# Attention over pairs of heads: value products of 512 columns, and eight wide buffers for exponentials and for pairs of parts

## The chip, the cores and the metric

The kernel runs on one core of a Trainium2 chip, as one launch. The metric is the device time of one execution, in microseconds (us). Names used below: PE is the matrix engine (TensorE), PEld its weight loads, DVE is VectorE, ACT is ScalarE, POOL is GpSimd, SP is the engine that issues most of the transfers.

## The reference, cut to what matters

One sequence of 1024 positions and 1024 channels goes through two layers in float32. Layer 0 mixes positions by grouped-query attention: 16 query heads of 64 channels share 4 key and value heads, four query heads to each. Layer 1 mixes by a gated unit, and each layer ends with a squared-ReLU MLP.

```python
q = apply_rope(rmsnorm(q.reshape(B, T, N_HEADS, HEAD_DIM), q_g), cos, sin)
k = apply_rope(rmsnorm(k.reshape(B, T, N_KV_HEADS, HEAD_DIM), k_g), cos, sin)
v = v.reshape(B, T, N_KV_HEADS, HEAD_DIM)
...
s = jnp.einsum('bqkgd,bskd->bkgqs', q_blk, k).astype(jnp.float32) * scale
p = jax.nn.softmax(s, axis=-1).astype(v.dtype)
return jnp.einsum('bkgqs,bskd->bqkgd', p, v)
```

## The kernel before, in words

**Precision.** Matrix operands are split into a high part, which the cast to `F32R` keeps, and a low part, the rest. A product of two matrices is then three products (high-high, high-low, low-high), or two where one side stands as a stack of both parts. ACT makes the high part by a copy with a cast, DVE the low one by a subtraction. `split`, `norm_hl` and `wo_prep` make such pairs.

**Memory.** `slot` gives a tile of 128 x 512 from a pool of 58 (tag `t`), `xslot` one of 16 (tag `x`), `wide` one of 128 x 1024; its tag `c` is a part of memory that `cut(4)` or `cut(8)` lays out anew for each stage, as four wide tiles or eight of half the size. A tile is given back after its last reader, and an instruction that is to write into a tile waits until one is free. In PSUM, `bank_x` has four buffers of 128 x 512, and `ps_s` two of 128 x 1024 for scores.

**Attention.** The work is cut into 64 units: a quarter of the queries (256 positions, as two blocks `j` of 128) by one head. The order is quarter `qq`, group `g` (the four heads that share values), head `h4`. For each unit there are these stages:

- `s_stage(u, j)`: 4 products of 512 columns give the scores of 128 queries against 1024 keys; DVE takes the negated maximum of each row (L955).
- `e_stage(u, j)`: ACT takes the exponential with that bias, into a wide buffer of tag `c`, and sums the rows (L961).
- `t_stage(u, sp)`: PE transposes a quarter of the keys (256) for both blocks `j` into one bank (L969); ACT casts it to the high part (L972).
- `h_stage(u, sp)`: DVE makes the low part (L978). Then the bank is free.
- `v_stage(u, sp)`: for each of two key blocks, PE multiplies the values (high and low stacked, 128 columns of weights) with the high and the low part, 256 columns each (L988), all into one accumulator of 128 x 256. After the last one, ACT copies its two halves of 64 partitions (L998, L1000): the rows that came from the high values and those from the low ones.
- `f_stage`: POOL adds the two (L1005).

Iteration `i` of the loop runs `s` and `e` of unit `i`, `t` and `h` of unit `i-1`, `v` and `f` of unit `i-2`. The order within an iteration is written out by hand in `ORDER`: a letter, which of the three units, and the number of the part.

```python
ORDER = "s00 v20 t10 q10 h10 t11 e00 s01 h11 t12 h12 v21 t13 e01 h13 v22 v23 q00 f20 m00"
```

`pin` keeps an instruction behind what was written before it for its engine, so that PE, ACT and DVE follow this string. `q` prepares queries (`q_stage` on POOL, every fourth iteration; `q_trans` on PE in the third and fourth of four). `m` is other work that is spread over the loop: `late_sums` and `late_rope` (the rest of the query norms, iterations 2 to 13), `mod_ahead` with its second half (a product with a row sum on DVE, L225, every fourth iteration), `slabs.step` (modulation vectors on POOL, with 16 products of one column at the end of each), and from iteration 53 on the output projection's preparation (`wo_sums`, `wo_prep`). `late_sums` squares on ACT (L636) and sums on DVE (L637).

Ahead of the loop the query projections of the second half of the positions (`qkv_mm`) run, with unit 0's scores and exponentials between them.

**Other stages.** The MLPs and the gated unit multiply by a scheme of seven block products in place of eight (`forms_a`, `forms_b`, `winograd`, `wino_v`, `Out`), whose 28 operand tiles each stand as a high and a low part. All these parts come from tag `t` before the change.

Of the kernel before, what the change touches and what calls it, by code (L numbers as in the profile page):

```python
# [18 lines left out]
P = 128  # L19
# [17 lines left out]
def encoder_kernel(ctx: ExitStack, tc: tile.TileContext, t: dict, out: bass.AP):  # L37
# [268 lines left out]
    def norm_hi(u, layer, which, k):  # L306
        hi = slot(F32R)
        hold(S.activation(hi, u, AF.Identity, bias=mod[:, layer, 3 * which, k : k + 1]))
        return hi

    def norm_lo(u, hi, layer, which, k):
        lo = slot(F32R)
        hold(V.scalar_tensor_tensor(lo, u, mod[:, layer, 3 * which, k : k + 1], f32(hi), ALU.add, ALU.subtract))
        return hi, lo

    def norm_hl(u, layer, which, k):
        return norm_lo(u, norm_hi(u, layer, which, k), layer, which, k)
# [45 lines left out]
    def forms_b(f, xt, layer, which, rb, order, apart=False):  # L363
# [10 lines left out]
        def forms(kt):  # L374
            if kt == 0:
                h(0)
            if kt < 3:
                h(kt + 1)
            b11, b21 = raw.pop(kt), raw.pop(kt + 4)
            t3[kt], t2 = slot(), slot()  # L380
            V.tensor_tensor(t3[kt], b22[kt], b12[kt], ALU.subtract)
            V.tensor_tensor(t2, b11, t3[kt], ALU.add)
            f[("6", kt)] = split(t2)
            left["5"].append((b12[kt], b11))
            left["4"].append((b21, t2))
            if not apart:
                subtract("54")
# [160 lines left out]
    if True:  # L548
# [323 lines left out]
        qkv_mm(2, 1, ps, hs1)  # L872
# [33 lines left out]
    def wo_prep(hf, dt):  # L906
# [4 lines left out]
        hi, lo = slot(F32R), slot(F32R)  # L911
# [20 lines left out]
    with ExitStack() as es:  # L932
# [13 lines left out]

        def s_stage(u, j):
# [10 lines left out]
        def e_stage(u, j):  # L958
            ps, mx = u.s[j]
            p_ = wide("c")  # L960
            pin(S.activation(p_, ps, AF.Exp, bias=mx,  # L961
                             accum_out=rowsum[:, 2 * u.qq + j, u.head : u.head + 1]))
            u.p.append(p_)

        def t_stage(u, sp):
            pt = bank_x("t")
            for s in range(2):
                for j in range(2):
                    pin(T.transpose(pt[:, (2 * s + j) * P : (2 * s + j + 1) * P],  # L969
                                    u.p[j][:, (2 * sp + s) * P : (2 * sp + s + 1) * P], ident))  # L970
            hi = slot(F32R)
            pin(S.copy(hi, pt))  # L972
            u.t.append((pt, hi))

        def h_stage(u, sp):
            pt, hi = u.t[sp]
            lo = slot(F32R)
            pin(V.tensor_tensor(lo, pt, f32(hi), ALU.subtract))  # L978
            u.pt.append((hi, lo))

        def v_stage(u, sp):
            if sp == 0:
                u.po = bank_x("o", (P, 256))
            hi, lo = u.pt[sp]
            for s in range(2):
                st = 2 * sp + s
                for part, src in ((0, hi), (1, lo)):
                    pin(T.matmul(u.po, vt[st][:, u.g * P : (u.g + 1) * P], src[:, s * 256 : (s + 1) * 256],  # L988
                                 start=st == 0 and part == 0, stop=st == 7 and part == 1))
            if sp < 3:  # L990
                return
            dt, hf = u.head // 2, u.qq // 2
            if (dt, hf) not in ot:
                ot[(dt, hf)] = slot()
            a = (u.head % 2) * 64
            b = 64 - a
            dst = ot[(dt, hf)][a : a + 64, (u.qq % 2) * 256 : (u.qq % 2) * 256 + 256]
            pin(S.copy(dst, u.po[b : b + 64]))  # L998
            src = slot()[a : a + 64, :256]
            pin(S.copy(src, u.po[a : a + 64]))  # L1000
            u.fin = (dst, src)

        def f_stage(u, _):
            dst, src = u.fin
            pin(G.tensor_tensor(dst, src, dst, ALU.add))  # L1005

        stages = dict(s=s_stage, e=e_stage, t=t_stage, h=h_stage, v=v_stage, f=f_stage)
        units = []
        for qq in range(4):
            for g in range(NKV):  # L1010
                for h4 in range(4):
                    u = Unit()
                    u.qq, u.g, u.h4, u.head = qq, g, h4, 4 * g + h4
                    u.s, u.p, u.t, u.pt = [], [], [], []
# [37 lines left out]
        for i in range(nu + 2):  # L1052
            u0 = units[i] if i < nu else None
            u1 = units[i - 1] if 0 < i <= nu else None
            u2 = units[i - 2] if i > 1 else None
# [4 lines left out]
            for op in ORDER.split():  # L1060
# [25 lines left out]
                else:  # L1086
                    u = (u0, u1, u2)[w]
                    if u and (i or f not in "se"):
                        stages[f](u, j)
# [11 lines left out]
    class Out:  # L1101
# [73 lines left out]
        def split_f(self, k):  # L1175
            self.f[k] = split(self.raw.pop(k))
# [592 lines left out]
SLOTS = {"t": 58, "x": 16, "w": 4, "s": 5}  # L1769
# [100 lines left out]
```

## Time and profile before

| what | value |
| --- | --- |
| three runs | 2610.8, 2616.09, 2616.37 us; median 2616.09 |
| the profiled execution | 2620.57 us, span 2618.8 us |
| granted PE clock, mean | 0.998 |
| busy share: PE, DVE, ACT, POOL | 99%, 83%, 55%, 27% |
| value products L988 | 1024 of 128 x 256, 165.3 to 548.5 us |
| transposes L969 | 1024 of 128 x 128 |
| score products L952 | 512 of 128 x 512, 153.2 to 534.1 us |
| casts L972 and low parts L978 | 256 each |

A row of the timeline has the start, the length, the engine, the line, the operation, what it writes and reads, its size and how many were merged; in brackets stands how long the engine sat idle before it and what ended that. A row of the groups has the busy time in all, the mean of one in ns, and the idle time before them. PE's busy time counts a matmul until its modelled end, and successive matmuls overlap, so the distance between starts is what counts.

### The profile page before, as it was taken

What the parts mean: (1) busy time and instruction counts of PE and PEld (TensorE: products, weight loads), DVE (VectorE), ACT (ScalarE), POOL (GpSimd) and SP (SyncE); (2) the same over time, 40 slices, a digit from 0 to 9 for tenths busy, and PEclk for the clock granted to TensorE, in tenths of its full rate; (3) what the DMA queues carried; (4) which work ended last, traced back from release to release, by engine and by line L of the source; (5) the groups of instructions that cost most, each with busy time, mean ns of one, the idle gap of its engine ahead of it and who ended that gap; (6) DMA issues with size and microseconds to landing.
All of it is one profiled execution on the core that took longest, in us unless ns stands there. A gap on an engine that the chain in (4) does not pass through costs nothing.

```text
span 2618.8 us, 37177 instructions
## 1 busy us (share of the span) xinstructions
PE 2593.0 (99%) x12808; PEld 2167.8 (83%) x12808; DVE 2179.8 (83%) x3281; ACT 1443.7 (55%) x2584; POOL 718.5 (27%) x527
## 2 busy tenths in 40 slices
PE   9999999999999999999999999999999999999999
PEld 7889999887788888888888888888788788888887
DVE  7878999887989999877987687778889977789974
ACT  4579999845644555345543454445456644455442
POOL 0237876433000005430122055442420000005400
PEclk9999999999999999999999999999999999999999
DMA  8100222233586798544243454568641554497461
GB/s 289 45 1 9 89 82 76 89 130 128 195 284 242 279 310 301 181 137 169 81 153 113 137 175 169 174 216 298 228 142 52 182 176 159 148 313 264 150 212 58
DMA packets 209327, 434.33 MB, mean 166 GB/s; under 512 B 23089, under 2 KB 35505, under 8 KB 209138
## 3 DMA queue, kind: packets, MB, share of 16 engines
q1 hardware_dynamic: 182258, 394.19, 44.7%
q10 hardware_dynamic: 26880, 37.76, 4.0%
q8 instruction: 101, 1.65, 0.3%
q14 instruction: 88, 0.72, 0.1%
HBM read 309.18 MB, written 122.68 MB: 165 GB/s over the span
## 4 chain that ended last, share of the span: by engine, by line
PE 83%; DVE 9%; DMA 3%; ACT 3%; issue 1%; POOL 1%; SPq 0%; DVEq 0%; ACTq 0%; POOLq 0%
PE w L474 10%; PE w L475 10%; PE w L476 10%; PE out L1215 9%; PE out L1216 9%; PE out L1217 9%; PE s L952 4%; PE o L988 4%; PE t L969 4%; PE v L1574 3%; PE v L1573 3%; PE v L1572 3%; PE mix L1679 1%; DVE t L334 1%; DMA t<-hf 1%
## 5 line engine op out<-in xcount | busy, mean ns | idle before, releaser
L1215 PE MATMUL out<-t,s 128*128 128x512 f32 x1232 | 480.1, 390 | 2.5 <-ACT t L333 2.5
L1216 PE MATMUL out<-t,s 128*128 128x512 f32 x1232 | 480.0, 390 | 1.6 <-DVE t L334 1.6
L1217 PE MATMUL out<-t,s 128*128 128x512 f32 x1232 | 479.4, 390 | 0.0
L474 PE MATMUL w<-t,s 128*128 128x512 f32 x1168 | 458.5, 394 | 1.8 <-DVE c L1683 1.2
L475 PE MATMUL w<-t,s 128*128 128x512 f32 x1168 | 455.2, 390 | 1.8 <-DVE t L334 1.8
L476 PE MATMUL w<-t,s 128*128 128x512 f32 x1168 | 454.7, 389 | 0.0
L334 DVE TENSOR_TENSOR t<-t,t 128x512 fp32r<-128x512 f32 x408 | 323.8, 804 | 27.4 <-ACT t L333 20.2
L333 ACT CAST t<-t 128x512 fp32r<-128x512 f32 x408 | 244.8, 617 | 121.1 <-DMA t<-hf 71.3
L1215 PEld LDWEIGHTS out<-t,s 128*128 128x128 f32 x1232 | 231.6, 188 | 51.6 <-ACT t L333 3.7
L1216 PEld LDWEIGHTS out<-t,s 128*128 128x128 f32 x1232 | 231.7, 188 | 50.4 <-DVE t L334 2.9
L1217 PEld LDWEIGHTS out<-t,s 128*128 128x128 f32 x1232 | 231.7, 188 | 48.4
L459 ACT CAST s<-w 128x512 fp32r<-128x512 f32 x292 | 173.5, 616 | 161.8 <-PE w L476 104.7
L474 PEld LDWEIGHTS w<-t,s 128*128 128x128 f32 x1168 | 219.4, 188 | 49.6 <-issue 3.5
L475 PEld LDWEIGHTS w<-t,s 128*128 128x128 f32 x1168 | 219.4, 188 | 48.7 <-DVE t L334 5.2
L460 DVE TENSOR_TENSOR s<-w,s 128x512 fp32r<-128x512 f32 x292 | 221.8, 766 | 43.7 <-ACT s L459 43.0
L1197 ACT CAST s<-t 128x512 fp32r<-128x512 f32 x240 | 148.4, 621 | 197.2 <-PE out L1217 143.8
L476 PEld LDWEIGHTS w<-t,s 128*128 128x128 f32 x1168 | 219.3, 188 | 45.3
L1198 DVE TENSOR_TENSOR s<-t,s 128x512 fp32r<-128x512 f32 x240 | 195.7, 816 | 63.9 <-ACT s L1197 63.1
L1183 POOL TENSOR_TENSOR w<-w,t 128x512 f32<-128x512 f32 x20 | 33.5, 1684 | 765.7 <-DVE t L334 345.8
L955 DVE TENSOR_REDUCE mx<-s 128x1 f32<-128x1024 f32 x128 | 156.2, 1221 | 27.2 <-PE s L952 25.5
L978 DVE TENSOR_TENSOR t<-t,t 128x512 fp32r<-128x512 f32 x256 | 164.2, 682 | 17.3 <-ACT t L972 16.2
L988 PE MATMUL o<-t,t 128*128 128x256 f32 x1024 | 163.5, 292 | 0.0
(259 smaller groups left out, 5060.7 us busy)
## 6 DMA issues: line engine op xcount, KB each, us to landing
t<-hf SPq DMA_DIRECT2D x320, 256.0 KB, 4.0
hf<-c SPq DMA_DIRECT2D x156, 256.0 KB, 3.1
w<-in_wi_dram SPq DMA_DIRECT2D x64, 512.0 KB, 4.3
hf<-c ACTq DMA_DIRECT2D x96, 256.0 KB, 2.3
w<-in_ada_dram SPq DMA_DIRECT2D x36, 512.0 KB, 4.1
x<-in_ada_dram SPq DMA_DIRECT2D x64, 256.0 KB, 5.9
t<-in_wm_dram SPq DMA_DIRECT2D x64, 256.0 KB, 4.9
wf<-w SPq DMA_DIRECT2D x64, 256.0 KB, 2.9
```

Source lines behind the costliest of these rows:

```text
L333: S.copy(hi, src)
L334: (eng or V).tensor_tensor(lo, src, f32(hi), ALU.subtract)
L459: S.copy(hi, src)
L460: V.tensor_tensor(lo, src, f32(hi), ALU.subtract)
L474: T.matmul(ps, hi[:, a], th, start=kt == 0, stop=False)
L475: T.matmul(ps, hi[:, a], tl, start=False, stop=False)
L476: T.matmul(ps, lo[:, a], th, start=False, stop=kt == 3)
L988: pin(T.matmul(u.po, vt[st][:, u.g * P : (u.g + 1) * P], src[:, s * 256 : (s + 1) * 256], start=st == 0 and part == 0, stop=st == 7 and pa ...
L1198: V.tensor_tensor(lo, src, f32(hi), ALU.subtract)
L1215: T.matmul(ps, hi[:, a], th, start=begin and kt == 0, stop=False, **g)
L1216: T.matmul(ps, hi[:, a], tl, start=False, stop=False, **g)
L1217: T.matmul(ps, lo[:, a], th, start=False, stop=end and kt == 3, **g)
```

## The change

Two heads of the same group become a `Pair`. Exponentials of both (four blocks of 128 queries) are collected in `pair.p`; tag `d` has eight wide buffers for them. A chunk `c` is one block of 128 keys: `t_stage` transposes it for all four blocks, and `v_stage` multiplies it in one product of 512 columns for the high and one for the low part, into an accumulator of 128 x 512. A pair has eight chunks. In iteration `i` (with `n = i // 2`) scores and exponentials are unit `i`'s; the transposes are chunks 0 to 3 (even `i`) or 4 to 7 (odd `i`) of pair `n-1`; the value products are chunks 5, 6 and 7 of pair `n-2` and chunk 0 of pair `n-1` (even), or 1 to 4 of pair `n-1` (odd). Copies and sums of a finished pair come at the end of an even iteration. `ORDER` is as before. Units 0 and 1 have their scores and exponentials ahead of the loop, between the halves of the last projections, and the loop starts at 2 and has one iteration more at its end.

Tag `t` shrinks from 58 to 42, and the eight wide buffers of `d` are new. Elsewhere `pair` hands out one of them as a high and a low part: in `norm_hl`, for the forms 6 and 5 of `forms_b`, in `Out.split_f`, and in `wo_prep` for the second half of the queries. The attention's results for the first half of the queries go to tag `c`, which is laid out by `cut(8)` before the loop.

```diff
+    def pair(dt=F32R):
+        w_ = wide("d", dt)
+        return w_[:, :512], w_[:, 512:]
...
-    def split(src, eng=None):
-        hi, lo = slot(F32R), slot(F32R)
+    def split(src, eng=None, home=None):
+        hi, lo = home() if home else (slot(F32R), slot(F32R))
...
-            f[("6", kt)] = split(t2)
+            f[("6", kt)] = split(t2, None, pair)
...
-                f[(q, kt)] = split(src[q][kt])
+                f[(q, kt)] = split(src[q][kt], None, pair if q == "5" else None)
...
-        hi, lo = slot(F32R), slot(F32R)
+        hi, lo = pair() if hf else (slot(F32R), slot(F32R))
...
-            p_ = wide("c")
+            p_ = wide("d")
...
+        def t_stage(pr, c):
             pt = bank_x("t")
-            for s in range(2):
-                for j in range(2):
-                    pin(T.transpose(pt[:, (2 * s + j) * P : (2 * s + j + 1) * P],
-                                    u.p[j][:, (2 * sp + s) * P : (2 * sp + s + 1) * P], ident))
+            for n in range(4):
+                pin(T.transpose(pt[:, n * P : (n + 1) * P], pr.p[n][:, c * P : (c + 1) * P], ident))
...
+        def v_stage(pr, c):
+            if c == 0:
+                pr.po = bank_x("o")
+            for part, src in enumerate(pr.t[c]):
+                pin(T.matmul(pr.po, vt[c][:, pr.g * P : (pr.g + 1) * P], src,
+                             start=c == 0 and part == 0, stop=c == 7 and part == 1))
+            if c == 7:
+                pr.src = slot()[:, :256]
+                if (pr.dt, pr.hf) not in ot:
+                    ot[(pr.dt, pr.hf)] = slot() if pr.hf else cslot()
+                pr.dst = ot[(pr.dt, pr.hf)][:, (pr.qq % 2) * 256 : (pr.qq % 2) * 256 + 256]
+                c_stage(pr, 0)
+
+        def c_stage(pr, i):
+            a, b = 64 * i, 64 - 64 * i
+            cols_ = slice(i * 256, (i + 1) * 256)
+            pin(S.copy(pr.dst[a : a + 64], pr.po[b : b + 64, cols_]))
+            pin(S.copy(pr.src[a : a + 64], pr.po[a : a + 64, cols_]))
+
+        def f_stage(pr):
+            c_stage(pr, 1)
+            pin(G.tensor_tensor(pr.dst, pr.src, pr.dst, ALU.add))
...
-        qkv_mm(2, 2, ps, hs1)
-        units[0].qst = nxt
-        s_stage(units[0], 0)
-        e_stage(units[0], 0)
-        qkv_mm(2, 3, ps, hs1, (0,))
-        s_stage(units[0], 1)
-        e_stage(units[0], 1)
-        qkv_mm(2, 3, ps, hs1, (1,))
+        qkv_mm(2, 1, ps, hs1, (1,))
+        for n, (kp, half) in enumerate(((2, 0), (2, 1), (3, 0), (3, 1))):
+            u = units[n // 2]
+            u.qst = nxt
+            s_stage(u, n % 2)
+            e_stage(u, n % 2)
+            qkv_mm(2, kp, ps, hs1, (half,))
+        qh = q_stage(units[4].qq, units[4].g)
+        cut(8)
...
-        for i in range(nu + 2):
+        qst, nxt = nxt, []
+        for i in range(2, nu + 3):
...
+                elif f in "th":
+                    if pr1:
+                        (t_stage if f == "t" else h_stage)(pr1, 4 * odd + j)
+                elif f == "v":
+                    c = (5, 6, 7, 0)[j] if not odd else 1 + j
+                    pr = prs[n - 2] if not odd and j < 3 and n > 1 else pr1 if odd or j == 3 else None
+                    if pr:
+                        v_stage(pr, c)
+                elif f == "f" and not odd and n > 1:
+                    f_stage(prs[n - 2])
...
-            self.f[k] = split(self.raw.pop(k))
+            self.f[k] = split(self.raw.pop(k), None, pair)
...
-SLOTS = {"t": 58, "x": 16, "w": 4, "s": 5}
+SLOTS = {"t": 42, "x": 16, "w": 4, "s": 5, "d": 8}
```

More of the change, by code (lines that the diff above doesn't have):

```diff
@@ L945, in encoder_kernel @@
             pass
+        class Pair:
+            pass
         def s_stage(u, j):
@@ L971, in t_stage, with h_stage @@
             hi = slot(F32R)
             pin(S.copy(hi, pt))
-            u.t.append((pt, hi))
-        def h_stage(u, sp):
-            pt, hi = u.t[sp]
+            pr.t[c] = (pt, hi)
+        def h_stage(pr, c):
+            pt, hi = pr.t[c]
             lo = slot(F32R)
             pin(V.tensor_tensor(lo, pt, f32(hi), ALU.subtract))
[L979 to L1008, printed above, removed]
+            pr.t[c] = (hi, lo)
+        def v_stage(pr, c):
[10 more added lines that the diff above has]
+                c_stage(pr, 0)
```

36 lines of the change are left out of this document (21 added, 15 removed).

## Prediction, before the change was run

> **What bounds the kernel now.** I read the page's first two parts, then the table by stage, the groups by line, and last the timeline of single attention iterations. The profiled execution took 2620.57 us (span 2618.8), 4.5 us above the median of the three runs shown, 2616.09; terms are worked out on the profile and added to the median.
>
> ```profile
> PE 2593.0 (99%) x12808; PEld 2167.8 (83%) x12808; DVE 2179.8 (83%) x3281; ACT 1443.7 (55%) x2584; POOL 718.5 (27%) x527
> ...
> PEclk9999999999999999999999999999999999999999
> ```
> ```profile
> core 0: us, PE busy (x) PEld busy (x) DVE busy (x) ACT busy (x) POOL busy (x), PEclk, DMA share, GB/s
> ...
> 260.00:300.00 40.00, 40.00 (x298) 37.07 (x297) 37.17 (x49) 37.34 (x75) 35.50 (x25) 1.00 0.28 93
> ```
> PE has no idle time worth the name, at full granted clock. In attention ACT and DVE are at 93% as well: PE is the bound with two engines close behind. Time is won only where PE's own work shrinks, and lost wherever PE is made to wait.
>
> One iteration, PE and DVE (the columns are start, length, engine, line, operation, count):
> ```profile
> 271.20 1.09 PE L952 MATMUL s<-x,t 128*128 128x512 f32 x4
> ...
> 272.13 0.64 PE L988 MATMUL o<-t,t 128*128 128x256 f32 x4
> ...
> 272.33 1.23 DVE L955 TENSOR_REDUCE mx<-s 128x1 f32<-128x1024 f32 x1 [0.22 <-PE s L952]
> 272.60 1.04 PE L969 MATMUL t<-ident,c 128*128 128x128 f32 x8
> ...
> 273.40 1.19 PE L952 MATMUL s<-x,t 128*128 128x512 f32 x4
> ...
> 273.86 0.69 DVE L978 TENSOR_TENSOR t<-t,t 128x512 fp32r<-128x512 f32 x1 [0.30 <-ACT t L972]
> ...
> 274.43 0.60 PE L969 MATMUL t<-ident,c 128*128 128x128 f32 x4
> ...
> 274.63 1.23 DVE L955 TENSOR_REDUCE mx<-s 128x1 f32<-128x1024 f32 x1
> 274.78 0.72 PE L988 MATMUL o<-t,t 128*128 128x256 f32 x4
> ...
> 275.34 0.60 PE L969 MATMUL t<-ident,c 128*128 128x128 f32 x4
> 275.70 1.20 PE L988 MATMUL o<-t,t 128*128 128x256 f32 x8
> 275.77 1.88 DVE L978 TENSOR_TENSOR t<-t,t 128x512 fp32r<-128x512 f32 x3
> ...
> 276.74 1.09 PE L952 MATMUL s<-x,t 128*128 128x512 f32 x4
> ```
> And of each line's own view the durations (smallest, median, largest, in ns):
> ```profile
> L988 PE MATMUL o<-t,t x1024: 274/283/416, 165.3 to 548.5; 128*128 128x256 f32 x171
> ...
> L969 PE MATMUL t<-ident,c x1024: 270/272/435, 161.4 to 540.1; 128*128 128x128 f32 x171
> ...
> L952 PE MATMUL s<-x,t x512: 389/397/628, 153.2 to 534.1; 128*128 128x512 f32 x171
> ```
> A matmul's printed length is its latency; what PE pays is the distance to the next. Four value products last 0.64 us and one 0.283, so they stand (0.64-0.283)/3 = 0.119 us apart; the score products (1.09-0.397)/3 = 0.231; the transposes (1.04-0.272)/7 = 0.110. 16 x 0.119 + 8 x 0.231 + 16 x 0.110 = 5.51 us, and the iteration from 271.20 to 276.74 is 5.54. No wait hides in it.
>
> **Part 1, wider value products.** 1024 products of 256 columns become 512 of 512 columns; the columns stay. No row shows this shape writing `o`. The nearest are the output products, which also add a chain into one bank with a new weight for each, and the score products of the same stage:
> ```profile
> 999.82 0.39 PE L1215 MATMUL out<-t,s 128*128 128x512 f32 x1
> 1000.05 0.39 PE L1216 MATMUL out<-t,s 128*128 128x512 f32 x1
> 1000.28 0.39 PE L1217 MATMUL out<-t,s 128*128 128x512 f32 x1
> 1000.50 0.39 PE L1215 MATMUL out<-t,s 128*128 128x512 f32 x1
> ```
> (1000.50-999.82)/3 = 0.227, against 0.231. Two narrow products cost 0.238, so a wide one saves 0.011 or 0.007: over 512 of them 5.6 or 3.6 us. I take 5.6, by the row that is nearest in form, and keep 3.6 as the other end. The Trainium skill (TensorE: Matmul & The Clock Gate, Back-to-back issue gap) gives N/2.4 + 2.5 ns, so 109.2 and 215.8 ns; by it a pair saves 2.5 ns, 1.3 us in all, and the sum below would be +13.6 instead of +9.3. The trace has 12 to 14 ns over the columns' time instead of 2.5, and it decides.
>
> **Part 2, where the first product of a pair stands.** ORDER is unchanged, but its four places for `v` now hold, in even iterations, chunks 5, 6, 7 of the old pair and, in the last place, chunk 0 of the new pair. Chunk 0 takes a new accumulator. The pool of `bank_x` has four buffers. At that moment one is the old pair's accumulator, whose chunk 7 has just been issued; its four ACT copies come only after the exponential. Of the four transposes of this iteration, the fourth has taken the first one's buffer, so chunks 1, 2 and 3 hold the other three. The first that comes free is chunk 1's, when DVE's `h11` has read it, and DVE can't be earlier: it is the first of the three L978 behind the maximum of `s01`. Read off the iteration above: three L978 in 1.88 us, one lasting 0.68, so the first ends at 275.77+0.68 = 276.45. The last place for `v` starts at 276.74 - 4 x 0.119 = 276.26, and 0.04 earlier with two shorter groups before it. A PE that waits for L978 starts 0.06 after its end (187.22+0.67 to 187.95):
> ```profile
> 184.28 0.63 ACT L636 ACTIVATE t<-t 128x512 f32<-128x512 f32 x1
> ...
> 184.95 0.69 DVE L637 TENSOR_REDUCE qss<-t 128x8 f32<-128x512 f32 x1 [1.38 <-ACT t L636]
> ...
> 187.22 0.67 DVE L978 TENSOR_TENSOR t<-t,t 128x512 fp32r<-128x512 f32 x1
> ...
> 187.95 0.66 PE L969 MATMUL t<-ident,c 128*128 128x128 f32 x4 [1.00 <-DVE t L978]
> ```
> So PE waits 276.51 - 276.22 = 0.29 us in every even iteration from 4 to 62, thirty of them. Behind it on PE stand the next scores, pinned, hence everything. In the kernel before, a new accumulator is first asked for after that last place (0.48) and the next `s00` (0.93), 1.4 us later, when the buffer has long been free.
>
> In some even iterations DVE is later, because `mod_ahead`'s second half runs just before them:
> ```profile
> L225 DVE SCALAR_TENSOR_TENSOR w<-w,s 128x1024 f32<-128x1024 f32 x10 | 12.2, 1216 | 0.0
> ```
> ```profile
> 305.88 1.22 DVE L225 SCALAR_TENSOR_TENSOR w<-w,s 128x1024 f32<-128x1024 f32 x1
> ...
> 310.49 1.87 DVE L978 TENSOR_TENSOR t<-t,t 128x512 fp32r<-128x512 f32 x3
> 310.94 1.09 PE L952 MATMUL s<-x,t 128*128 128x512 f32 x4
> ```
> There the first L978 ends at 311.17 and the place starts at 310.94-0.48 = 310.46, so the wait is 0.71+0.06+0.04 = 0.81. Ten such updates, of which two fall into iterations that the slab sums lengthen anyway: 8 x 0.81 + 22 x 0.29 = 12.9 us. Bounds: 6 if only half of it stays on PE because the order in time gives another buffer, 16 if DVE lags further.
>
> **Part 3, four copies at once.** The accumulator's copies (L998, L1000) were two per iteration and are four in every second one; their number stays.
> ```profile
> 272.23 0.36 ACT L998 COPY t<-o 64x256 f32<-64x256 f32 x1
> ...
> 272.60 0.37 ACT L1000 COPY t<-o 64x256 f32<-64x256 f32 x1
> ...
> 273.24 1.08 ACT L972 CAST t<-t 128x512 fp32r<-128x512 f32 x2 [0.27 <-PE t L969]
> ```
> 0.75 us more ACT in even iterations, 0.75 less in odd ones. ACT waits 0.27 for PE at the cast that follows, so chunk 4's cast is up to 0.5 late (0.75 behind a query's cast), and PE itself is 0.29 late there. Chunk 7's transpose needs chunk 4's buffer: it starts at 275.34, and that buffer's L978 ended at 273.86+0.69 = 274.55, 0.79 earlier. So it costs nothing, narrowly. Where `late_sums` runs (iterations 2, 4, 6, 8), DVE already waits 1.38 for the square behind these copies, and PE then 1.00. In 4, 6 and 8 the square now stands behind four copies: +0.75, less the 0.29 that PE is late itself, about +0.5 each; in 2 there are no copies yet, -0.5. Together +1, bounds 0 to 3.
>
> **Part 4, the rest.** The sum of the halves on POOL is half as many instructions on 128 partitions; PE waits for none of them. The projections interleaved with four scores and exponentials before the loop are the same matmuls in another order, and two `d` buffers of the second norm's pairs are free before each exponential needs one: nothing; without that cover PE would wait for the first maximum (1.23). At the end, two iterations without scores replace one; the output projection stands ready to fill them. Slots `t`: 42 instead of 58, while 16 that the forms held move to `d` and eight accumulators to `c`. I count from the code about 41 live in iterations 2 to 8 and 44 to 45 in 61 to 63, where the quotients for the first half take 16: there a cast waits until a chunk's product frees a slot. The broadcast `bc` in 56 to 62 also wants a second buffer behind chunk 0. I set +1 for both, bounds 0 to 6. In the other stages pairs in `d` take the slots they had in `t`; Out's ninth pair waits for PE to finish with the first, but it is needed four units later: nothing, +-2. No DMA is added or moved.
>
> **Sum:** -5.6 + 12.9 + 1 + 1 = +9.3 us: 2629.9 on the profile, about 2625 on the median.
>
> **Rivals.** (a) *The bank is no wait.* If chunk 0 finds a buffer free, PE keeps running and the change is worth its matmuls: -5.6 to -3.6 and +0 to 2, so 2610.5 to 2614.5. It decides as soon as `h11` ends 0.3 us earlier relative to PE. For it: 0.29 is small and DVE waits 0.22 and 0.30 us in the rows above. Against it: those waits are for PE and ACT and stand in the chain already counted. (b) *Half the wait.* The late iterations settle at the short wait: 30 x 0.29 = 8.7, or half of that, and the sum is 0 to +5: 2616 to 2621. (c) *Slots bind.* Casts wait for slots in 2 to 8 and 55 to 63 as well; one chunk's product, 0.5 us, to one iteration's wait of 1 in some 16 iterations adds 8 to 16: 2633 to 2641. For it: attention was near its 58. Against: the need exceeds 42 by my count only late. (d) *Weight loads bound PE*, and half of those for values go:
> ```profile
> L988 PEld LDWEIGHTS o<-t,t 128*128 128x128 f32 x1024 | 139.0, 190 | 5.5
> ```
> Half of 139.0 is 69.5 us: 2547. Against it: four loads of 0.19 would need 0.76 where four products take 0.64, so loads overlap, and products alone fill the iteration. The Trainium skill (Perfetto Trace Analysis, Identifying the Most-Contended Engine) calls the share of weight loads a good measure of this engine; no row here follows it.
>
> **How the numbers follow.** Forecast, 2621 to 2630: 0.43. (a) 0.25, of which half is below 2610.9. (b) 0.19. (c) 0.12. (d) 0.01. A measurement tells about 0.2% (5.2 us) from no change. Faster: 0.12 + 0.01 = 0.13, and 0.01 for what I have not seen: 0.14. Same: 0.12 + 0.18 = 0.30. Slower: 0.56. The range 2610 to 2635 leaves out (d), most of (c) and a little at the lower end, some 0.15; the forecast's own range is 2621 to 2630.
>
> **What would show it.** Wide value products 0.227 to 0.231 apart. In even iterations the first `o` product of a pair behind an idle of about 0.3, and 0.8 where L225 ran, put down to DVE L978 (as idle of PE or of its weight load); none in odd ones. Two iterations without transposed queries take 11.2 us instead of 11.08. Between 184 and 220, DVE's wait for the square over 2 us. If the first `o` product never waits, (a) holds and part 2 is wrong; if casts L972 wait for `o` products near 520, (c). The prediction is wrong in size if other stages, untouched in my sum, move by more than 2 us.

## The result, and the profile after

The change makes the kernel slower: 2648.06 us (median of five, 2645.17 to 2653.13) against 2615.65 (median of five, 2610.8 to 2616.37), a ratio of 1.0133 with a 95% interval of 1.0117 to 1.0150. The forecast was 2625 with a range of 2610 to 2635. The sign was right; 23 us of the 32 that were lost were not in it.

The profiled execution of the kernel after took 2653.13 us (span 2651.2, 32.4 longer than before's). Its page and its table by stage, in the lines that answer to those of before:

```profile
PE 2603.6 (98%) x12296; PEld 2138.0 (81%) x12296; DVE 2188.9 (83%) x3281; ACT 1456.1 (55%) x2584; POOL 694.9 (26%) x495
...
260.00:300.00 40.00, 36.46 (x206) 29.39 (x205) 34.48 (x43) 31.56 (x62) 25.17 (x15) 0.96 0.22 68
```

In the attention PE is now busy 36.46 of 40 us instead of all 40, at a mean clock of 0.96 instead of 1.00, while DVE and ACT also do less. Nobody is the bound there: they wait for each other. The timeline of PE over three iterations (16, 17 and 18) and the start of the fourth shows where:

```profile
255.73 1.08 PE L960 MATMUL s<-x,t 128*128 128x512 f32 x4
...
261.07 0.71 PE L991 MATMUL o<-t,t 128*128 128x512 f32 x2 [0.19 <-DVE t L984]
261.61 1.09 PE L960 MATMUL s<-x,t 128*128 128x512 f32 x4
...
267.09 1.08 PE L960 MATMUL s<-x,t 128*128 128x512 f32 x4
...
272.90 0.66 PE L976 MATMUL t<-ident,d 128*128 128x128 f32 x4 [1.25 <-DVE t L984]
273.31 0.71 PE L991 MATMUL o<-t,t 128*128 128x512 f32 x2
274.72 1.14 PE L991 MATMUL o<-t,t 128*128 128x512 f32 x2 [0.70 <-DVE t L984]
275.66 1.91 PE L960 MATMUL s<-x,t 128*128 128x512 f32 x4
277.36 1.01 PE L991 MATMUL o<-t,t 128*128 128x512 f32 x2
```

The even iteration 16 takes 261.61 - 255.73 = 5.88 us, the odd 17 takes 5.48; both took 5.53 before. That is the forecast's mechanism: a wait ahead of chunk 0, put down to DVE. Iteration 18 takes 8.57 us. Before, that iteration took 5.89. It holds two waits of 1.25 and 0.70 us, and behind them the score products stand (277.36-275.66)/4 = 0.425 apart instead of 0.23. The value products' own view confirms the first kind, thirty times:

```profile
L991 PE MATMUL o<-t,t x512: 387/397/776, 174.4 to 591.2; 128*128 128x512 f32 x171
...
  PE o L991: 22.1, 30
  DVE t L984: 9.8, 30
```

What makes iteration 18 long stands on DVE and POOL. First DVE, then POOL, in the kernel after:

```profile
266.15 1.87 DVE L984 TENSOR_TENSOR t<-t,t 128x512 fp32r<-128x512 f32 x3
267.95 2.96 DVE L229 SCALAR_TENSOR_TENSOR w<-w,s 128x1024 f32<-128x1024 f32 x1
...
271.03 1.22 DVE L963 TENSOR_REDUCE mx<-s 128x1 f32<-128x1024 f32 x1
```
```profile
263.80 0.74 POOL L1008 TENSOR_TENSOR c<-t,c 128x256 f32<-128x256 f32 x1 [6.10 <-ACT t L1004]
264.51 2.85 POOL L203 TENSOR_SCALAR w<-w,cols 128x1024 f32<-128x1024 f32 x1
267.45 2.39 POOL L204 TENSOR_TENSOR s<-s,w 128x1024 f32<-128x1024 f32 x1
```

The update L229 lasts 2.96 us instead of 1.22. It ends at 270.91, about 1.1 us after POOL's sum L204 (267.45 + 2.39 = 269.84), as if it did nothing while POOL worked and then ran its own 1.1 to 1.2. In the kernel before, at the same place, POOL came later (DVE, then POOL):

```profile
260.31 1.22 DVE L225 SCALAR_TENSOR_TENSOR w<-w,s 128x1024 f32<-128x1024 f32 x1
```
```profile
261.33 0.78 POOL L1005 TENSOR_TENSOR t<-t,t 64x256 f32<-64x256 f32 x1 [4.88 <-ACT t L1000]
262.21 2.85 POOL L199 TENSOR_SCALAR w<-w,cols 128x1024 f32<-128x1024 f32 x1
265.15 2.41 POOL L200 TENSOR_TENSOR s<-s,w 128x1024 f32<-128x1024 f32 x1
```

There the update had ended at 261.53. POOL had to wait 4.88 us for ACT's copies before its sum of the two halves, and went on to the slab only afterwards. In the kernel after that sum exists in even iterations alone; in the odd ones POOL waits for nothing and starts the slab's two instructions 3.4 us ahead of the update, so that L204 begins 0.5 us before it.

The third loss is ahead of the attention: PE's longest wait of the whole execution, at the sums of squares of the second half's norm.

```profile
85.25 1.12 PE L284 MATMUL ss<-ident,t 128*128 128x128 f32 x4 [5.80 <-DVE t L268]
```
ACT makes those squares (L264) one at a time there, with 0.7 to 1.0 us of waiting between; in the kernel before three came in a row (the second fence):
```profile
76.48 0.63 ACT L264 ACTIVATE t<-x 128x512 f32<-128x512 f32 x1
77.93 0.63 ACT L264 ACTIVATE t<-x 128x512 f32<-128x512 f32 x1 [0.83 <-DVE t L268]
...
82.45 0.63 ACT L264 ACTIVATE t<-x 128x512 f32<-128x512 f32 x1 [1.00 <-DVE t L268]
```
```profile
72.05 1.67 ACT L260 ACTIVATE t<-x 128x512 f32<-128x512 f32 x3
```

By start times of the same instruction in both traces the difference runs as follows. The scores of unit 11 come 6.6 us later than before (226.41 against 219.82), those of unit 54 33.7 later (501.96 against 468.26), those of unit 63 39.1, the end of the output projection 43.0 (678.4 against 635.4), and the end of the last output products 32.4 (2647.3 against 2614.9). So the stages behind the attention, untouched in the sum, gave 10.6 back.

### The profile page after: what moved, and what is told of

Its sections match the earlier page's. It is cut to its first block, busy times and chain, and to the rows that moved or that the text cites. A ratio compares the mean times of both kernels' runs of the same rounds, so it can differ in the third digit from the quotient of the medians.

```text
span 2651.2 us, 36208 instructions
## 1 busy us (share of the span) xinstructions
PE 2603.6 (98%) x12296; PEld 2138.0 (81%) x12296; DVE 2188.9 (83%) x3281; ACT 1456.1 (55%) x2584; POOL 694.9 (26%) x495
## 4 chain that ended last, share of the span: by engine, by line
PE 82%; DVE 11%; ACT 2%; DMA 2%; issue 1%; POOL 0%; SPq 0%; DVEq 0%; ACTq 0%
PE out L1234 11%; PE out L1235 11%; PE out L1236 11%; PE w L479 10%; PE w L480 10%; PE w L481 10%; PE s L960 3%; PE o L991 3%; PE v L1593 3%; PE v L1592 3%; PE v L1591 3%; PE t L976 2%; DVE mx L963 2%; PE mix L1698 2%; DVE t L984 2%
## 5 line engine op out<-in xcount | busy, mean ns | idle before, releaser
L1234 PE MATMUL out<-d,s 128*128 128x512 f32 x1232 | 479.7, 389 | 0.0
L1236 PE MATMUL out<-d,s 128*128 128x512 f32 x1232 | 479.3, 389 | 0.0
L1235 PE MATMUL out<-d,s 128*128 128x512 f32 x1232 | 479.3, 389 | 0.0
L479 PE MATMUL w<-t,s 128*128 128x512 f32 x816 | 321.4, 394 | 0.2 <-DVE c L1702 0.2
L480 PE MATMUL w<-t,s 128*128 128x512 f32 x816 | 318.7, 391 | 1.7 <-DVE t L339 1.6
L481 PE MATMUL w<-t,s 128*128 128x512 f32 x816 | 317.7, 389 | 0.0
L339 DVE TENSOR_TENSOR d<-t,d 128x512 fp32r<-128x512 f32 x332 | 270.4, 834 | 7.1 <-ACT d L338 6.9
L1236 PEld LDWEIGHTS out<-d,s 128*128 128x128 f32 x1232 | 231.3, 188 | 48.4
L1234 PEld LDWEIGHTS out<-d,s 128*128 128x128 f32 x1232 | 231.3, 188 | 48.1 <-ACT d L338 0.4
L1235 PEld LDWEIGHTS out<-d,s 128*128 128x128 f32 x1232 | 231.3, 188 | 47.6
L1217 DVE TENSOR_TENSOR s<-t,s 128x512 fp32r<-128x512 f32 x240 | 189.4, 791 | 63.9 <-ACT s L1216 63.8
L338 ACT CAST d<-t 128x512 fp32r<-128x512 f32 x332 | 203.1, 620 | 40.7 <-DMA t<-hf 29.7
L984 DVE TENSOR_TENSOR t<-t,t 128x512 fp32r<-128x512 f32 x256 | 164.1, 682 | 23.8 <-ACT t L978 23.5
L480 PEld LDWEIGHTS w<-t,s 128*128 128x128 f32 x816 | 153.3, 188 | 35.3 <-DVE t L339 5.2
L991 PE MATMUL o<-t,t 128*128 128x512 f32 x512 | 171.4, 428 | 9.8 <-DVE t L984 9.8
L479 PEld LDWEIGHTS w<-t,s 128*128 128x128 f32 x816 | 153.3, 188 | 33.2 <-issue 1.7
L481 PEld LDWEIGHTS w<-t,s 128*128 128x128 f32 x816 | 153.2, 188 | 31.4
```

Source lines behind the costliest of these rows:

```text
L479: T.matmul(ps, hi[:, a], th, start=kt == 0, stop=False)
L480: T.matmul(ps, hi[:, a], tl, start=False, stop=False)
L481: T.matmul(ps, lo[:, a], th, start=False, stop=kt == 3)
L991: pin(T.matmul(pr.po, vt[c][:, pr.g * P : (pr.g + 1) * P], src, start=c == 0 and part == 0, stop=c == 7 and part == 1))
L1234: T.matmul(ps, hi[:, a], th, start=begin and kt == 0, stop=False, **g)
L1235: T.matmul(ps, hi[:, a], tl, start=False, stop=False, **g)
```

## The experiments

Two theories stood at first for the long iterations. *Collision*: POOL's sum of two operands and DVE's update with two operands (all in SBUF, where the tiles of all tags stand) exclude each other. *Lateness*: DVE has no slack where a bank waits for it, and any 1.2 us at that place would cost as much.

**1. The update moved to an even iteration.**

```diff
-                    if late_mods and i % 4 == 1:
+                    if late_mods and i % 4 == 2:
```


> The kernel after, with one edit: the second half of the modulation update (L229, DVE, ten times) runs at the end of the even iterations i % 4 == 2 instead of the odd ones i % 4 == 1. There it stands in an iteration in which POOL first waits for the sum of the two halves (L1008), and so for ACT's copies, before it goes on to the slab's products. Theory (collision): in the kernel after, POOL's two-input sum L204 starts about 0.5 us ahead of L229, and L229 or the small sum behind it ends only with it (2.96 instead of 1.21 us in 6 of 10, a wait of 2.2 us behind it in others); PE then loses about 1.6 us and has a lower granted clock for several us. With the edit L229 takes 1.2 us ten times, the iterations around it last 5.9 to 6.7 instead of 8.1 to 8.9, the granted clock stays above 0.97 in 270:320, and the time is 20 to 27 us below the kernel after: 2621 to 2628. Rival 1 (lateness alone): any update of 1.2 us on DVE costs these iterations about 2 us, since DVE has no slack where a bank waits for it; then the iterations stay near 8 us and the time within 6 us of 2648. Rival 2 (what the prediction had, 0.81 instead of 0.29 of wait): L229 is short in both, and the gain is 8 x 0.5 = 4 us.

Measured: 2631.6 us (2630.42 to 2633.68), 16.5 less than the kernel after; ratio to before 1.0061 (1.0048 to 1.0073). All ten updates are short, and the clock is back (by stage; before, after and this run, 250 to 440 us):

```profile
L229 DVE SCALAR_TENSOR_TENSOR w<-w,s x10: 1211/1214/1224, 273.1 to 468.0; 128x1024 f32<-128x1024 f32 x10
```
```profile
250.00:440.00 190.00, 190.00 (x1410) 176.40 (x1409) 173.93 (x228) 173.51 (x344) 143.43 (x108) 1.00 0.25 82
250.00:440.00 190.00, 178.21 (x1035) 146.01 (x1035) 163.09 (x203) 155.42 (x310) 112.47 (x77) 0.97 0.20 67
250.00:440.00 190.00, 186.91 (x1118) 154.75 (x1117) 166.21 (x219) 168.19 (x335) 125.59 (x85) 1.00 0.22 73
```
Of the seven iterations that took 8.1 to 8.9 us, six take 6.20 to 6.21. The seventh, iteration 50, took 10.75, and that is why the gain stayed below the 20 to 27 expected: the ninth update now waited 3.71 us for its transfer, and PE behind it 3.38, with wide products 0.5 to 0.6 apart afterwards.

**2. One operand instead of two, at the same place.** This tells collision from lateness: the reduction is as long as an undisturbed update, and POOL's work stays where it was. The kernel leaves out the product with the condition and the bias.

```diff
-            pin(V.scalar_tensor_tensor(raw, raw, 1.0, cond[0], ALU.mult, ALU.mult, accum_out=acc))
-            V.tensor_tensor(acc, acc, adab[:, layer, j, k : k + 1], ALU.add)
+            pin(V.tensor_reduce(acc, raw, AX.X, ALU.add))
             if j in (1, 4):
-                mod_scale(layer, j // 3, k)
+                V.tensor_scalar(amod[:, layer, j // 3, k : k + 1], acc, 1.0, None, ALU.add)
```


> The kernel after, with the update at its place, but with one operand in SBUF instead of two: L229 is a sum over the 1024 columns alone (TENSOR_REDUCE, also 128x1024), and the two small operations behind it become one with one operand. The product with the condition and the bias are left out, so its output is not the reference's. Theory (collision of a two-operand DVE instruction with POOL's): the reduction lasts 1.1 to 1.3 us in all ten, also where POOL's L204 runs over it, the ten iterations last 5.9 to 6.8 us, and the time is 20 to 27 us below the kernel after. Rival (lateness alone): the reduction is as long as an undisturbed update, the iterations stay near 8 us, and the time stays within 6 us of 2648. Rival (any DVE instruction collides): the reduction too lasts near 3 us where L204 started ahead of it, and nothing changes.

Measured: 2629.97 us (2625.53 to 2631.83), 18.1 less than the kernel after.

```profile
L229 DVE TENSOR_REDUCE mod<-w x10: 1207/1207/1209, 271.7 to 485.9; 128x1 f32<-128x1024 f32 x10
```
```profile
268.27 2.85 POOL L203 TENSOR_SCALAR w<-w,cols 128x1024 f32<-128x1024 f32 x1
271.21 2.39 POOL L204 TENSOR_TENSOR s<-s,w 128x1024 f32<-128x1024 f32 x1
```
The first reduction started at 271.69, 0.48 us behind POOL's sum, exactly the place at which the two-operand update took 2.96; it took 1.21. Five of the ten stood so, and none was longer than 1209 ns. Lateness alone is excluded: 1.2 us at that place cost nothing that shows (iteration 18, behind an update, takes 6.21, and iteration 14, with no update before it, takes as much). From unit 11 to unit 54 this run is 20.7 us shorter than the kernel after (254.86 against 275.55): that is the price of the collision there, clock included.

**3. The collision made in the kernel before.** POOL's sum of the halves is put behind the slab's step.

```diff
-ORDER = "... v22 v23 q00 f20 m00"
+ORDER = "... v22 v23 q00 m00 f20"
```


> The kernel before, with the last two entries of the order exchanged: the slab's step and the update (m00) stand ahead of the sum of halves (f20) on POOL, so POOL no longer waits for ACT's copies before it goes on to a slab's product. Theory (POOL's sum in each iteration kept the slab's products off the update): L225 now meets L200 in some of the ten, there lasts up to 3 us instead of 1.22, and the kernel before itself becomes 5 to 25 us slower, 2621 to 2640, with a lower granted clock behind those places. Rival (the order on POOL does not matter, it is the bank that makes the update dear): L225 may be long, but the time stays within 5 us of 2616.

Measured: 2627.52 us (2626.21 to 2630.49), 10.6 above before; ratio 1.0042 (1.0029 to 1.0055).

```profile
L225 DVE SCALAR_TENSOR_TENSOR w<-w,s x10: 1212/2541/2542, 258.4 to 476.5; 128x1024 f32<-128x1024 f32 x10
```
Eight of the ten updates last 2.5 us. Seven of them lengthen their iteration, from 5.89 to 7.22 us (the last from 6.08 to 7.42); the eighth falls into one that takes 5.90 in both. From unit 11 to 54 that is 7 x 1.33 = 9.3 us, and the traces differ by 257.81 - 248.44 = 9.4 there. So the order on POOL alone, without pairs, makes a loss of this kind, half as large. One part of the theory was wrong: the clock did not fall. PE had a single wait of 1.15 us in such an iteration here, not two.

**4. Chunk 0 behind the next scores.** This tests the wait that the forecast was built on.

```diff
-                    c = (5, 6, 7, 0)[j] if not odd else 1 + j
-                    pr = prs[n - 2] if not odd and j < 3 and n > 1 else pr1 if odd or j == 3 else None
+                    if odd and j == 0:
+                        v_stage(pr1, 0)
+                    c = 5 + j if not odd else 1 + j
+                    pr = pr1 if odd else prs[n - 2] if j < 3 and n > 1 else None
```


> The kernel after, with the first two value products of a pair (chunk 0) moved from the last place for v of an even iteration to the first place for v of the odd iteration that follows, where four products then stand. Theory (the bank): chunk 0's new accumulator waits for h11 on DVE, 0.43 us in 22 plain iterations and more where the update ran; moved past the next scores it finds the buffer free. Plain even iterations take 5.45 to 5.5 instead of 5.88 to 5.90 us, PE's idle ahead of the value products (9.8 us, and 22.1 of its weight loads) falls to near 0, and the time is 30 x 0.43 = 13 us below the kernel after, up to 18 if the update's iterations gain too: 2630 to 2635. Rival (DVE is the bound): DVE's own work of an even iteration is as long as the iteration, so PE waits as long at another place; then even iterations stay at 5.8 and the time moves by less than 4 us.

Measured: 2645.81 us (2644.59 to 2648.37), 2.3 less than the kernel after and within the spread of both. The wait ahead of the value products is gone, and half of it came back elsewhere. The two answers are those of L991 and L976 (who kept the line's engine idle, us and times, PE and its weight loads counted together):

```profile
  DVE t L984: 0.3, 1
...
  ACT t L1004: 10.1, 22
```
In plain pairs of iterations two take 4.99 + 5.92 = 10.91 us instead of 5.88 + 5.48, so 0.45 less, as expected. In pairs with transposed queries they take 5.33 + 6.76 = 12.09 and took 6.21 + 5.86 = 12.07: there the queries' transposes take a bank as well, and the transposes behind them now wait for ACT to copy the old accumulator out (in 11 places, each counted once for PE and once for its weight loads). The bank theory holds for the place; the expected 13 us did not come, and I read these rows to say that the four banks are short in those iterations whichever product comes first. In the profiled run 7.3 us were gained by the last scores (565.83 against 573.15). Nine plain pairs gain 0.4 to 0.5 each, 3.9 in all. The pairs that begin at 4, 8, 28 and 40, which hold late norms or the slab's products, gain 0.1 or less, and 2.4 lie in iterations 54 to 57. The rival, that DVE is the bound, is out by the plain pairs.

**5. The squares in the idle buffers `d`.**

```diff
-        def add(self, xk, eng=V):
-            sq = slot()
+        def add(self, xk, eng=V, home=slot):
+            sq = home()
...
-            sq1.add(xs1[k])
+            sq1.add(xs1[k], V, lambda: pair(F32)[0])
...
```


> The kernel after, with the squares of the second half's first norm in the eight buffers d, which are idle at that time, instead of slots t. Theory (slots): with 42 slots the squares and the casts of the weights go one at a time as products free a slot, and PE stands still for 5.8 us ahead of L284 at 85.25, with a lower clock behind it; with the squares elsewhere that idle goes, the first score products start 5 to 7 us earlier than at 156.5, and the time is 5 to 7 us below the kernel after: 2641 to 2643. Rival (the weights' casts bind, not the squares): the idle moves to the projections behind it, and the time moves by less than 2 us.

Measured: 2639.42 us (2638.38 to 2641.85), 8.6 less than the kernel after.

```profile
81.24 1.11 PE L284 MATMUL ss<-ident,d 128*128 128x128 f32 x4 [2.70 <-DVE d L268]
```
The idle falls from 5.80 to 2.70 us and the first scores stand at 151.0 instead of 156.5: 5.5 us of the gain are this, by one trace of each. A start taken from one trace is good to a few us only: in the five runs whose work ahead of the scores is that of the kernel after (it, runs 1, 2, 4 and 10) the first scores come at 155.9 to 160.3, in the three with squares in `d` (runs 5, 6 and 7) at 149.6 to 151.0. That the edit brings the scores forward is clear of this spread; how much of the 8.6 it makes there is not. What is left of the idle comes from the weights' casts, which still wait for slots (the longest time 3.97 us, for DVE's L801, which builds a table in `t`).

**6. and 7. The edits together.** First 1, 4 and 5 at once; then the same with the update's load and second half moved once more:

```diff
-                    if late_mods and i % 4 == 2:
+                    if late_mods and i % 4 == 0:
...
-                    if i % 4 == 3 and 12 <= i < 52:
+                    if i % 4 == 2 and 12 <= i < 52:
```


> The kernel after with three edits at once, each run alone before: the update at the end of i % 4 == 2, chunk 0 at the front of the odd iteration, the squares of the second half's first norm in d. Alone they were worth 16.5, 2.3 and 8.6 us of 2648.06. If they are separate costs (theory), the sum is 27.4: 2620.7, between 2614 and 2624, so slower than the kernel before by 0 to 0.3%. Rival (shared slack: what one frees, the next had already hidden): 2626 to 2631.

> As the one before, but the update's load stands in i % 4 == 2 (14 to 50) and its second half in i % 4 == 0, two iterations behind the load as in the kernels before and after, where no slab product is started in that iteration. With the update in i % 4 == 2 the load was held three iterations, and PE once waited 3.4 us at 465 for a DVE that waited 3.7 for that transfer, with a lower clock behind it. Theory: this wait goes, L229 stays at 1.2 us ten times, and the time is 4 to 8 us below the run before: 2610 to 2616, about that of the kernel before. Rival (the transfer is late for another cause): the wait stays, and so does the time, 2617 to 2624.

Measured: 2626.61 us (2621.18 to 2629.78) and 2628.55 us (2624.6 to 2628.74), ratios to before 1.0037 (1.0025 to 1.0049) and 1.0040 (1.0028 to 1.0052). The three edits gave 21.5 us, not 27.4. The profiled execution was this run's fastest, and in it PE still waited 3.8 us, until 457.0, behind the late ninth transfer. The second version got rid of that wait and walked into the collision again, in four of ten:

```profile
L229 DVE SCALAR_TENSOR_TENSOR w<-w,s x10: 1211/1282/2782, 254.8 to 471.3; 128x1024 f32<-128x1024 f32 x10
```
Its expectation said that no slab product is started in that iteration. That is so, but the one of the iteration before it had not yet ended: L204 was still running, begun 0.7 to 1.1 us earlier.

**8. and 9. The storage alone.** The kernel after with the attention of the kernel before: single heads, products of 256 columns, its loop and its start. Storage stays as after: 42 slots, `d`, accumulators of the first half in `c`.

```diff
-            pr.po = bank_x("o")
+            u.po = bank_x("o", (P, 256))
...
             p_ = wide("d")
...
-        for i in range(2, nu + 3):
+        for i in range(nu + 2):
```


> The kernel after with the pairs of heads undone: attention by single heads, with the value products of 256 columns, the projections ahead of it and the loop as in the kernel before. What stays of the change is the storage: 42 slots t, eight d for the exponentials and for the pairs of high and low parts, the first half's accumulators in c. Theory (attention by pairs costs what the traces say: 20.5 us between the scores of units 0 and 54 in the run with the update moved aside and 35 in the kernel after; the storage costs about 6.5 ahead of the scores by the slots and gives about 10.5 back behind the attention): four iterations take 22.8 us as in the kernel before, L229's form lasts 1.2 us ten times, and the time is 2616.9 + 6.5 - 10.5 = 2613, between 2607 and 2618. Rival (42 slots bind in the attention too): casts wait for slots there, and the time is 2622 or more. Rival (the gain behind the attention belongs to the later start, not to the storage): it stays away, 2622 to 2625.

> As the one before, and the squares of the second half's first norm in d. That edit was worth 8.6 us alone in the kernel after. Theory: the stall of PE ahead of L284 shrinks from 6 to 3 us as it did there, and the time is 2605 (2600 to 2610), 0.3 to 0.6% below the kernel before. Rival (the gain behind the attention stays away): 2614 to 2618, no change.

(In the first of these expectations the 20.5 and 35 us were misread: from the scores of unit 0 to those of unit 54 the traces give 14.4 us over before for run 1 and 30.5 for the kernel after.) Measured: 2621.67 us and, with the squares in `d`, 2618.55; ratios 1.0016 (1.0007 to 1.0026) and 1.0002 (0.9993 to 1.0011). In both, four iterations in a row take 22.8 us as before and every update 1.21 to 1.22, with the clock at 1.00, so 42 slots do not bind in the attention (the row is run 9's):

```profile
250.00:440.00 190.00, 190.00 (x1413) 176.46 (x1411) 173.62 (x227) 173.47 (x345) 143.49 (x107) 1.00 0.24 79
```
Ahead of it they do: the first scores come at 163.4 in the first of the two and at 159.1 in the second, against 153.2. So the storage costs 10.2 us there, more than the 6.5 that I had read from the kernel after, and the squares are 4.3 of it. Both figures come from single traces, with the spread named above. Behind the attention this storage gave back 5.3 us (from +11.9 at the end of the output projection to +6.6 at the end), half of what the kernel after gave back. The version with the squares in `d` equals the kernel before; none of the versions beats it.

**10. The output products' forms back in `t`.**

```diff
-            self.f[k] = split(self.raw.pop(k), None, pair)
+            self.f[k] = split(self.raw.pop(k))
```


> The kernel after, with the forms of the output products back in slots t (Out.split_f without a pair; d stays empty there). From 1766.9 to 2001.7 the kernel before took 234.8 us, the kernel after 229.7 in the same stage (1805.8 to 2035.5), and before had three waits of PE (2.36 at 1867.8, 1.1 at 1981.4, 1.96 at 2035.6) that are gone. Theory (pairs in d keep the products' forms from taking the slots that the next blocks' loads need): with 42 slots for all, the stage is as long as before or longer, 234 to 245, and the time 4 to 15 us above the kernel after. Rival (the waits went by chance of the timing): the stage stays at 229.7 and the time within 3 us of 2648.

Measured: 2650.11 us (2647.27 to 2654.06), and the gated unit's output stage is as short as with pairs. By stage, the rows are before, after, this run, and run 8 (with the pairs in `d`, but attention by single heads):

```profile
1766.90:2001.70 234.80, 231.92 (x1018) 191.00 (x1017) 205.32 (x289) 119.83 (x209) 62.21 (x41) 0.99 0.58 200
1805.80:2035.50 229.70, 229.65 (x1017) 189.88 (x1016) 206.53 (x289) 121.83 (x209) 63.21 (x41) 1.00 0.59 203
1807.70:2037.20 229.50, 229.50 (x1017) 190.02 (x1016) 208.53 (x288) 119.17 (x209) 60.77 (x41) 1.00 0.59 199
1777.10:2010.50 233.40, 231.36 (x1017) 191.05 (x1016) 206.43 (x290) 121.95 (x209) 63.12 (x41) 0.99 0.58 201
```
My theory that pairs in `d` gave this stage its 5 us falls. From its first output product to its last the stage takes 229 to 230 us in all eight kernels with attention by pairs and 233 to 235 in the four without, whatever the storage; why a stage 1200 us later should care is open.

## Why the prediction was wrong, step by step

**Part 1 (wider value products)** was right in kind. Odd iterations, which hold no new wait, take 5.45 to 5.48 instead of 5.53. That is 0.05 to 0.08 for eight products, some 4 us in all, nearer to the other end of 3.6 than to the 5.6 that I took.

**Part 2 (chunk 0 waits for its bank)** was right in place, cause and count, and too small in plain iterations. Between them lies 5.88 - 5.47 = 0.41 to 0.43 us instead of 0.29. The row above shows 0.19 of idle on PE, which is less than PE loses, since its busy time counts a product to its modelled end: single products show chunk 0's first 0.58 to 0.60 behind the one before it in plain iterations, where 0.23 would do, so 0.36. Of what the forecast lacked, most is the restart: in each of the thirty places PE starts 0.14 to 0.15 behind the end of L984, and the forecast took 0.06 from a transpose.

The price of 0.81 behind an update, in eight iterations, did not hold as it was derived. In run 2, where the update's place in DVE's row is taken by 1.21 us that do not collide (and 0.2 us of small operations behind it are left out), PE's idle ahead of chunk 0 is 0.18 to 0.20 in 28 of the 30 iterations and 0.38 in two, so the update pushes almost nothing. The kernel after does show 0.7 of idle there, in seven iterations, near the forecast's sign of 0.8, but that is the collision: the likeness is luck. Luck is also in the sum. Run 2, which has this wait and no collision, is 254.86 - 248.44 = 6.4 us longer than before from unit 11 to 54; with the 3 us that the wide products save in those 43 iterations the wait is worth 9 there; the forecast's terms give 7 x 0.81 + 14 x 0.29 = 9.7 for the same iterations, too much in seven and too little in fourteen.

The step that failed is the one on the iterations with the update. I took L225 at 1.22 us from its row and asked only where it would push L978: 8 x 0.81. But the change altered what runs beside it. **Part 4** said of POOL's sum of halves that "PE waits for none of them", and so priced its going at nothing. The sum was not a wait of PE; it was what held POOL back until the update was done. Half as many sums let POOL run ahead into the update: 20.7 us between units 11 and 54 by run 2, of which 16.5 and 18.1 came back at once in runs 1 and 2 on the medians, and run 3 makes a loss of the same kind, 10.6, in the kernel before. The rule was at hand. The Trainium skill (SBUF — State Buffer, Who interferes with whom) says that a DVE instruction with two operands in SBUF contends with a GpSimd instruction that reads SBUF, that one with a single operand doesn't, and that whoever issues first keeps the shared ports to its end. The trace agrees where POOL runs its two-operand sum: 2.96 us behind L204, 1.21 with one operand (run 2), 1.21 where the update came first. It does not agree for POOL's one-operand L203, which reads SBUF too: an update that ran under it took 1.21 (rows in the last section). What the rows tell is that L204 collides and L203 does not; that it takes two operands on both sides is my reading.

**Part 3 (four copies at once)** held: the sums of the query norms wait 2.30 us for the square instead of 1.38 where the profile shows it, as said.

**Part 4, slots.** I counted the need in iterations 2 to 8 and 61 to 63 and set +1. Casts hardly waited there (0.9 us for value products in all, in run 1), so rival (c) is out as it was put. The need that binds is 80 us earlier, in the projections, which I did not count: 10.2 us by run 8, on one trace. The forecast said "nothing" of that stage. Part of the 10.2 is hidden in the difference at unit 11, 6.6: at the same unit's scores the pairs are further behind with transposes and products. For the same reason the stretch behind the last scores is 4.0 us longer, with 40 transposes and 28 wide products in it instead of 24 and 44 narrow ones, (40-24) x 0.110 + (28-22) x 0.231 = 3.1.

**Other stages, "nothing, +-2".** They gave 10.6. By runs 7 to 10 about half follows the storage, about half goes with attention by pairs and is unexplained. That the two big misses, 20.7 and 10.2, met an unforeseen gain of 10.6 is why the total was off by no more than 23.

Adding up, on the two profiles: 6.6 to unit 11, 27.1 from there to unit 54 (20.7 collision, 6.4 for the bank less the wider products), 5.4 to unit 63, 4.0 to the end of the output projection, -10.6 behind it: 32.5 from the rounded terms, against 32.4. The 5.4 near the end of the loop were not taken apart; run 1 has 1.3 there and run 2 has 0.6, so I put most of it down to what follows the collision.

## What to carry to other kernels

An instruction that nobody waits for can still be what keeps its engine out of another's way: before removing one, ask what runs earlier once it is gone, and whether that is, as here, a two-operand POOL instruction beside a two-operand DVE instruction. When slots are cut, count the live tiles in every stage that the pool serves, the first one too, not in the stage that is being changed. When a wait for a bank is moved past other work, look at who takes the bank next; with four banks and a late copy-out the wait came back in half of the places.

## What the runs showed of the hardware that I had not expected

A two-operand DVE instruction of one column waits as fully as a long one. In the kernel after, where the update escaped the collision, the small sum behind it took 2.22 us instead of 0.16. POOL's one-operand L203, which was running when the update began and for 0.9 us of it, did not delay it; the small sum ended with the two-operand L204 (DVE, then POOL):

```profile
397.68 1.21 DVE L229 SCALAR_TENSOR_TENSOR w<-w,s 128x1024 f32<-128x1024 f32 x1
398.82 0.08 DVE L229 DVE_READ_ACCUMULATOR w<-w,s 128x1 f32 x1
398.94 2.22 DVE L230 TENSOR_TENSOR mod<-mod,cols 128x1 f32<-128x1 f32 x1
```
```profile
395.72 2.85 POOL L203 TENSOR_SCALAR w<-w,cols 128x1024 f32<-128x1024 f32 x1
398.65 2.49 POOL L204 TENSOR_TENSOR s<-s,w 128x1024 f32<-128x1024 f32 x1
```

PE's clock fell behind waits that were short, but not each time. In the kernel after, seven iterations hold a wait of 1.2 to 1.7 us and another of 0.7, with 1.1 us of work between. Behind four of them the granted clock is 0.50 for 3.4 us (in the first, products of 512 columns stand 0.425 apart instead of 0.23); behind the other three it stays at 1.00. One of each kind, behind waits of 1.25 and 0.70 and of 1.21 and 0.70:

```profile
274.80:278.20 3.40, 3.40 (x8) 2.57 (x9) 1.56 (x3) 2.23 (x6) 1.05 (x2) 0.50 0.01 4
328.50:331.90 3.40, 3.40 (x22) 2.96 (x23) 2.50 (x4) 3.15 (x8) 1.05 (x2) 1.00 0.00 0
```

What decides between them is open. After a single wait of 1.15 to 1.34 us (run 3, seven times) the clock did not fall. The Trainium skill (TensorE: Matmul & The Clock Gate, HAM oscillation — how this bites in real kernels) puts the bound at gaps of about 3.4 us; the traces here show the half clock behind shorter ones, two close together, in four cases of seven.
